# Scheduling priorities in four levels, and the FFN down weights' sums made during FFN up

## The chip, the cores and the metric

One Trainium2 chip, of which the kernel uses one core. The metric is the device time of one execution in microseconds (us), as the median of several runs. A core has the engines TensorE (PE in the rows, its weight loads PEld), VectorE (DVE), ScalarE (ACT) and GpSimd (POOL), and SyncE (SP), which here issues nearly all DMA transfers. Every engine takes its instructions in the order in which they stand in its own queue and stops at one whose inputs aren't there.

## The reference

One layer of a streaming encoder for 1024 tokens of width 1024, in float32. The change touches its last part, the gated MLP:

```python
h = rms_norm(x, norm2_w[l])
up = h @ ffn_w_up[l]                       # 1024 x 6144
gate, val = jnp.split(up, [D_FF], axis=-1) # D_FF = 3072
gate = causal_depthwise_conv(gate, ffn_conv_w[l], ffn_conv_b[l])
x = x + (jax.nn.gelu(gate) * val) @ ffn_w_down[l]
return rms_norm(x, norm_f_w)
```

Ahead of it stand a norm, an input projection of width 8192, a retention branch and a recurrent branch (RG-LRU) with an output projection each, a gated merge, and a projection with a residual.

## The kernel before

**Products.** Every large matrix product is made of jobs. A job takes a weight block of 1024 x 256 (four tiles A11, A12, A21, A22 of 128 x 512) and an operand of 1024 x 1024 (tiles B11 to B22, each in four pieces of 128 x 512). Each float32 tile is split in two (`split`, L164): ScalarE casts a high part (L167), VectorE subtracts it for the low part (L168), and each product is three passes of matmuls. A plain job (`mm_std`) has 96 matmuls. Most jobs are fast ones (`mm_fast`, L377), by Strassen's scheme in Winograd's form: 7 products of 12 matmuls, in the order A11·B11, S1·T1, S2·T2, A12·B21, S3·T3, A22·T4, S4·B22, where S1 to S4 are sums of weight tiles and T1 to T4 sums of operand tiles (T1 = B12-B11, T2 = B22-T1, T3 = B12-B22, T4 = B21-T2). A fast job uses three banks X, Y, Z of PSUM. Where one product's result goes on in two sums, ScalarE copies the bank to SBUF (`keep`, L399, the copy is L402) before the next product adds to it; a result is finished by VectorE adding a bank to such a copy (`total`, L411, the addition is L413). The sixth and seventh products of a job come after the first of the next one.

**Weight blocks.** `preps` (L224) makes the split tiles of a job and its sums S1 to S4 (L246, L249, L255, L262) from raw tiles that `loads` (L199) brings by SP (L208). `pump` keeps up to seven blocks and six raw tiles ready, from 22 tiles W of their own.

**Operands.** Generators in a queue `builders` load an operand's pieces, split them and form T1 to T4. `operand` (L983) does the 16 plain pieces, `tsets` (L539) loads the same 16 again and subtracts (L544, L547, L550, L552), one piece j of all of T1 to T4 after the other. `build` (L285) advances them after every product by a budget of 3, if 20 of the 81 tiles U are free; `need` (L295) forces them where TensorE's instruction is written. An operand with its sums holds 64 of the 81 tiles.

**FFN.** FFN up has 24 jobs (one plain, 23 fast). After job i `post_ff(i)` (L1207) does the convolution (L1212 to L1217), the gelu (L1218) and the gating (L1219) and stores to the DRAM tile `ff_d` by GpSimd's queue (L1220). FFN down contracts over 3072 in three thirds g of 1024. There the activations from `ff_d` are the weight blocks, and the operand is a third of the down weights: `down_op(g)` (L1226) loads it from `w_dn` (L1230) and builds it with its sums. It is queued for g = 0 when job 22 of FFN up ends, later in each third's third job (`down_post`, L1311). Each third has one plain and three fast jobs; the partial results go through the DRAM tile `x1_d` (loads L1260, stores L1274; the rows call it x_d). The last third ends with the final norm.

**Order.** The program's text gives every instruction a number as its priority. A planner that runs ahead of time, with an estimate of each duration, lays down each engine's queue: whenever the engine is free in its plan, it takes the ready instruction with the lowest number. `hp()` (L161) is a context that lowers the numbers by 1500. It stands around the preparation of weight blocks (`pump`, after the first job), operand builders (`build`, `need`), `keep`'s copies, `total`'s additions, and the loads and splits of the output projection's weights (L1166). All else has its plain number: `post_ff`, the stores, and the work in the queue `back`, from which `advance` takes a budget of 1 after every product.

Of the kernel before, what the change touches and what calls it, by code (L numbers as in the profile page):

```python
# [11 lines left out]
F32 = mybir.dt.float32  # L12
# [5 lines left out]
P = 128  # L18
D = 1024
T = 1024  # L20
KT = 8
TH = 512
# [64 lines left out]
class Units:  # L87
# [11 lines left out]
    def get(self, dt=F32):  # L99
        i = self.q.popleft()  # L100
        self.count += 1
        t = self.pool.tile(self.shape, dt, tag=f"{self.name}{i}", name=f"{self.name}{i}_{self.count}")
        self.at[id(t)] = (i, t)
        return t
# [12 lines left out]
RATE = 1.0  # L117
BRATE = 3.0
RESERVE = 20
FAST_RO = 0  # L120
RO_T = 9
FAST_LO = 3
# [6 lines left out]
def tile_trunk_layer(ctx, tc, x, xt, positions, params, consts, normf, w_in, w_ro, w_lo,  # L129
# [23 lines left out]
    sg_d = pdr.tile([2, KT, P, T], F32, tag="sg", name="sg_d")  # L153
    t1_d = pdr.tile([KT, P, T], F32, tag="t1", name="t1_d")
    x1_d = pdr.tile([T, D], F32, tag="x1", name="x1_d")
    ff_d = pdr.tile([3, 8, 2, P, 4, P], F32, tag="ff", name="ff_d")

    def pc(name, i):
        return par[:, PCOL[name] + i:PCOL[name] + i + 1]

    def hp():  # L161
        return tc.high_priority(offset=1500)

    def split(src, get=get):  # L164

        hi, lo = get(F32R), get(F32R)
        S.copy(hi, src)  # L167
        V.tensor_sub(lo, src, hi.bitcast(F32))  # L168
        return hi, lo
# [114 lines left out]

    def build(budget, reserve=RESERVE):  # L285

        with hp():
            while builders and budget > 0 and len(U) >= reserve:
                c = next(builders[0], None)
                if c is None:  # L290
                    builders.popleft()
                else:
                    budget -= c

    def need(op, key):  # L295
        with hp():
            while key not in op:
                if next(builders[0], None) is None:
                    builders.popleft()
        return op[key]  # L300
# [76 lines left out]
    def mm_fast(jb, op):  # L377
        X, Y, Z = psg.get(), psg.get(), psg.get()

        def prod(bank, an, bn, first):  # L380
            pump((jb, an))
            w = jb.blk[an]
            n = 0
            for j in range(4):
                c = slice(128 * j, 128 * j + 128)
                for a, b in PASSES:
                    PE.matmul(bank, w[a][:, c], need(op, (bn, j))[b], start=first and n == 0, stop=n == 11,  # L387
                              skip_group_check=True)
                    n += 1
            W.put(*w)  # L390
            state["blocks"] -= 1
            if jb.last:
                for j in range(4):
                    drop(op.pop((bn, j)))
            pump()
            build(BRATE)
            advance(RATE)

        def keep(bank):  # L399
            u = get()  # L400
            with hp():
                S.copy(u, bank)  # L402
            return u

        def more(u, m, c):
            if jb.pre is not None and (m, c) in jb.pre:
                acc = jb.take(m, c)
                V.tensor_add(u, u, acc)
                put(acc)

        def total(u, bank, m, c):  # L411
            with hp():
                V.tensor_add(u, bank, u)  # L413
            jb.emit(m, c, u, u)

        prod(X, "A11", "B11", True)
        s1 = keep(X)
        yield
        jb.ask(0, 0)
        prod(Z, "S1", "T1", True)  # L420
        prod(X, "S2", "T2", False)
        u2 = keep(X)
        more(s1, 0, 0)
        jb.ask(1, 1)
        prod(Y, "A12", "B21", True)
        total(s1, Y, 0, 0)
        psg.put(Y)
        jb.ask(1, 0)
        prod(X, "S3", "T3", False)
        u3 = keep(X)  # L430
        more(u3, 1, 1)
        total(u3, Z, 1, 1)
        yield
        jb.ask(0, 1)
        prod(X, "A22", "T4", False)
        jb.emit(1, 0, X, None)
        psg.put(X)
        more(u2, 0, 1)
        prod(Z, "S4", "B22", False)
        total(u2, Z, 0, 1)  # L440
        psg.put(Z)

# [88 lines left out]
    def reads(fetch, keys, ahead):  # L531

        keys, got = deque(keys), deque()
        while keys or got:
            while keys and len(got) <= ahead:
                got.append(fetch(*keys.popleft()))
            yield got.popleft()
# [445 lines left out]
    def operand(op, fetch, sums=True):  # L983

        keys = [(n, j) for n in ("B11", "B21", "B12", "B22") for j in range(4)]
        for key, t in zip(keys, reads(fetch, keys, 3)):
            op[key] = split(t)
            put(t)
            yield 0.6
        if sums:  # L990
            yield from tsets(op, fetch)
# [234 lines left out]
    def down_op(g):  # L1226
        def fetch(n, j):
            t = get()
            kh, c = int(n[1]) - 1, int(n[2]) - 1
            SY.dma_start(t, w_dn[8 * g + 4 * kh + j, :, TH * c:TH * c + TH])  # L1230
            return t

        yield from operand(dop[g], fetch)

    builders.append(tsets(h2, lambda n, j: keep2[n, j]))
    NF = FF // P
    dop = [{} for _ in range(3)]

    def up_post(i):
        def fn():  # L1240
            if i == NF - 2:
                builders.append(down_op(0))
            post_ff(i)
        return fn

    run([Job(pair_src(w_up, i), h2, emit_to(gv), up_post(i), fast=i >= STD_U, last=i == NF - 1,
# [132 lines left out]
```

## Time and profile before

| | |
|---|---|
| median of 3 runs | 1673.02 us (1672.82 to 1676.43) |
| profiled execution, its own time | 1675.42 us |
| its span, first to last instruction | 1673.6 us |
| TensorE's mean granted clock | 0.994 of full speed |
| busy: PE, PEld, DVE, ACT, POOL | 97%, 80%, 77%, 53%, 2% |
| bytes read, written in HBM | 164.8 MB, 54.5 MB |

The span has these parts: input projection and both branches to about 640 us, the branches' output projections to 846, the merged projection to 950, FFN up to about 1400, FFN down to the end. An engine is busy while it executes; the time ahead of an instruction in which its engine stood still is its idle time, and the profile names who released it. Idle time matters on the engine that sets the pace. A timeline row merges instructions of one line that follow each other.

### The profile page before, as it was taken

The numbers are of one execution on the slowest core, as the hardware profiler recorded it, in microseconds if no ns is written. First come the engines' busy times: TensorE is split into PE (matmuls) and PEld (weight loads), VectorE is DVE, ScalarE is ACT, GpSimd is POOL, SyncE is SP. The second block draws the span as 40 slices with busy tenths as digits, with TensorE's granted clock in tenths as the row PEclk, the third lists the DMA queues.
The fourth block names the chain that finished last, engine by engine and source line by source line (L and its number), as shares of the span: only waits on it lengthen the run. The fifth ranks groups of instructions, "written<-read, shape, count | busy, mean of one in ns | idle before, by whom it ended". The sixth has DMA issues, their size and how long they took to land.

```text
span 1673.6 us, 21183 instructions
## 1 busy us (share of the span) xinstructions
PE 1627.2 (97%) x7224; PEld 1332.6 (80%) x7224; DVE 1289.9 (77%) x2366; ACT 886.4 (53%) x1480; POOL 40.7 (2%) x60
## 2 busy tenths in 40 slices
PE   8999999999999999999999999999999999999997
PEld 6888788888888877887778788888888887777776
DVE  8998768666888889857862796777767777878886
ACT  7654444535678877753530564444444455444554
POOL 0001000000000000000000000000000000000000
PEclk9999999999999999999999999999999999999999
DMA  7243212131333348656463022222222237687851
GB/s 293 89 154 97 86 54 89 51 95 45 113 114 105 122 140 267 210 166 232 154 209 107 32 95 82 82 82 82 89 82 82 92 122 229 224 260 243 260 193 76
DMA packets 120524, 225.97 MB, mean 135 GB/s; under 512 B 14048, under 2 KB 14176, under 8 KB 120416
## 3 DMA queue, kind: packets, MB, share of 16 engines
q1 hardware_dynamic: 116192, 210.99, 39.1%
q0 software_dynamic: 4224, 13.64, 2.1%
q8 instruction: 56, 0.92, 0.2%
q14 instruction: 52, 0.43, 0.1%
HBM read 164.80 MB, written 54.53 MB: 131 GB/s over the span
## 4 chain that ended last, share of the span: by engine, by line
PE 50%; DVE 8%; DMA 6%; ACT 3%; issue 2%; SPq 0%; DVEq 0%; ACTq 0%
PE g L387 36%; PE g L330 7%; PE g L1182 4%; DMA u<-w_dn 2%; DVE u L168 2%; PE a L814 2%; DVE w L168 1%; DMA w<-ff_d 1%; DMA x_d<-u 1%; DVE u L797 1%; ACT u L167 1%; DVE u L413 1%; DMA u<-u_d 1%; PE a L513 0%; DMA u<-w_out 0%
## 5 line engine op out<-in xcount | busy, mean ns | idle before, releaser
L387 PE MATMUL g<-u,w 128*128 128x512 f32 x5124 | 1204.7, 393 | 20.1 <-ACT u L402 9.7
L387 PEld LDWEIGHTS g<-u,w 128*128 128x128 f32 x5124 | 958.9, 188 | 224.6 <-ACT u L402 14.8
L167 ACT CAST w<-w 128x512 fp32r<-128x512 f32 x471 | 291.3, 621 | 359.7 <-PE g L387 280.6
L168 DVE TENSOR_TENSOR w<-w,w 128x512 fp32r<-128x512 f32 x471 | 322.6, 686 | 90.0 <-ACT w L167 85.4
L330 PE MATMUL g<-u,w 128*128 128x512 f32 x960 | 227.2, 394 | 2.8 <-ACT u L167 2.8
L167 ACT CAST u<-u 128x512 fp32r<-128x512 f32 x232 | 139.3, 620 | 150.1 <-DVE u L552 16.1
L330 PEld LDWEIGHTS g<-u,w 128*128 128x128 f32 x960 | 181.3, 190 | 41.9 <-ACT u L167 3.2
L168 DVE TENSOR_TENSOR u<-u,u 128x512 fp32r<-128x512 f32 x232 | 154.5, 687 | 38.8 <-ACT u L167 25.9
L413 DVE TENSOR_TENSOR u<-g,u 128x512 f32<-128x512 f32 x183 | 125.6, 686 | 57.0 <-PE g L387 43.5
L402 ACT COPY u<-g 128x512 f32<-128x512 f32 x183 | 106.4, 582 | 73.8 <-PE g L387 73.7
L1182 PE MATMUL g<-u,u 128*128 128x512 f32 x384 | 90.1, 392 | 2.5 <-ACT u L167 1.6
L1182 PEld LDWEIGHTS g<-u,u 128*128 128x128 f32 x384 | 71.3, 188 | 18.4 <-ACT u L167 2.0
L1215 DVE SCALAR_TENSOR_TENSOR u<-u,par,u 128x511 f32<-128x511 f32 (+1 forms) x96 | 71.6, 747 | 6.2 <-ACT u L1212 5.5
L1220 POOL DMA_DIRECT2D ff_d<-u x48 | 36.2, 753 | 1271.0 <-DVE u L1219 1271.0
L246 DVE TENSOR_TENSOR w<-w,w 128x512 f32<-128x512 f32 x61 | 42.1, 690 | 20.6 <-DMA w<-w_up 12.6
L814 PE MATMUL a<-u,u 128*128 128x512 f32 x192 | 48.8, 394 | 4.3 <-ACT u L167 3.5
L1184 DVE TENSOR_TENSOR u<-g,u 128x512 f32<-128x512 f32 x16 | 11.1, 691 | 49.3 <-PE g L1182 49.3
L1212 ACT ACTIVATE u<-u,par 128x512 f32<-128x512 f32 x48 | 39.1, 817 | 15.7 <-DVE u L413 15.7
L814 PEld LDWEIGHTS a<-u,u 128*128 128x128 f32 x192 | 35.5, 188 | 14.3 <-ACT u L167 5.6
L249 DVE TENSOR_TENSOR w<-w,w 128x512 f32<-128x512 f32 x61 | 42.0, 688 | 0.9
L262 DVE TENSOR_TENSOR w<-w,w 128x512 f32<-128x512 f32 x61 | 41.9, 686 | 0.4
L255 DVE TENSOR_TENSOR w<-w,w 128x512 f32<-128x512 f32 x61 | 41.8, 685 | 0.3
(173 smaller groups left out, 1151.2 us busy)
## 6 DMA issues: line engine op xcount, KB each, us to landing
w<-w_in SPq DMA_DIRECT2D x112, 256.0 KB, 2.7
w<-w_up SPq DMA_DIRECT2D x96, 256.0 KB, 2.6
u<-w_dn SPq DMA_DIRECT2D x96, 256.0 KB, 4.0
u<-x_d SPq DMA_DIRECT2D x56, 256.0 KB, 5.3
x_d<-u SPq DMA_DIRECT2D x48, 256.0 KB, 3.3
ff_d<-u POOLq DMA_DIRECT2D x48, 256.0 KB, 2.5
w<-ff_d SPq DMA_DIRECT2D x48, 256.0 KB, 3.8
u<-x SPq DMA_DIRECT2D x32, 256.0 KB, 5.3
```

The costliest lines, as they stand in the source:

```text
L167: S.copy(hi, src)
L168: V.tensor_sub(lo, src, hi.bitcast(F32))
L246: V.tensor_add(s1, a21, a22)
L249: V.tensor_sub(s1, s1, a11)
L262: V.tensor_sub(s1, a12, s1)
L330: PE.matmul(ps[h], w[a][:, c], o[b], start=n == 0, stop=n == 23)
L387: PE.matmul(bank, w[a][:, c], need(op, (bn, j))[b], start=first and n == 0, stop=n == 11, skip_group_check=True)
L402: S.copy(u, bank)
L413: V.tensor_add(u, bank, u)
L814: PE.matmul(ps, wg[g][a][:, cs], xs[k][b], start=q == 0, stop=q == 5)
L1182: PE.matmul(ps, o[a][:, 128 * t:128 * t + 128], wo[k][b], start=n == 0, stop=n == 23)
L1215: V.scalar_tensor_tensor(c[:, s:], src[:, :TH - s], w, c[:, s:], ALU.mult, ALU.add)
```

## The change

`hp` takes its offset as an argument, and there are four levels beside the plain one: 3000 (NOW) for `keep`'s copies and `total`'s additions, 1500 as before for weight blocks and the output projection's weights, 800 (OLD) for `post_ff` of the last three jobs of FFN up, 400 (SOON) for the operand builders.

The sums of the down weights move. After every second job of FFN up `down_sums(g, j)` is queued in `back`, 12 in all: it loads four tiles of `w_dn`, makes the four sums and stores them to a new DRAM tile `td_d`. `down_op` loads and splits the 16 plain pieces as before, and then, in the order T1, T2, T3, T4, loads the 16 sums from `td_d` and splits them, with a budget of 0.6 for each piece where the four pieces of one j had 4.8 together.

```diff
+NOW, SOON, OLD = 3000, 400, 800
+    td_d = pdr.tile([3, 4, 4, P, TH], F32, tag="td", name="td_d")
-    def hp():
-        return tc.high_priority(offset=1500)
+    def hp(offset=1500):
+        return tc.high_priority(offset=offset)
@@ build, need
-        with hp():
+        with hp(SOON):
@@ keep, total
-            with hp():
+            with hp(NOW):
@@ down_op
-        yield from operand(dop[g], fetch)
+        yield from operand(dop[g], fetch, False)
+
+        def sums(n, j):
+            t = get()
+            SY.dma_start(t, td_d[g, int(n[1]) - 1, j])
+            return t
+
+        keys = [(f"T{i}", j) for i in (1, 2, 3, 4) for j in range(4)]
+        for key, t in zip(keys, reads(sums, keys, 3)):
+            dop[g][key] = split(t)
+            put(t)
+            yield 0.6
+
+    def down_sums(g, j):
+
+        b = {}
+        for kh in range(2):
+            for c in range(2):
+                b[kh, c] = get()
+                SY.dma_start(b[kh, c], w_dn[8 * g + 4 * kh + j, :, TH * c:TH * c + TH])
+        yield 1.0
+        t = get()
+        V.tensor_sub(t, b[0, 1], b[0, 0])
+        ST.dma_start(td_d[g, 0, j], t)
+        put(b[0, 0])
+        yield 1.0
+        V.tensor_sub(b[0, 1], b[0, 1], b[1, 1])
+        ST.dma_start(td_d[g, 2, j], b[0, 1])
+        put(b[0, 1])
+        yield 1.0
+        V.tensor_sub(b[1, 1], b[1, 1], t)
+        ST.dma_start(td_d[g, 1, j], b[1, 1])
+        put(t)
+        yield 1.0
+        V.tensor_sub(b[1, 0], b[1, 0], b[1, 1])
+        ST.dma_start(td_d[g, 3, j], b[1, 0])
+        put(b[1, 0], b[1, 1])
@@ up_post
-            post_ff(i)
+            with hp(OLD) if i >= NF - 3 else nullcontext():
+                post_ff(i)
+            return down_sums(i // 8, i % 8 // 2) if i % 2 == 0 else None
```

(`ST` is SP here, as `GQ` is False.)

## Rows read from the trace of the kernel before

**Rows 1.** The page, busy time by engine: us (share of the span) xinstructions.

```profile
PE 1627.2 (97%) x7224; PEld 1332.6 (80%) x7224; DVE 1289.9 (77%) x2366; ACT 886.4 (53%) x1480; POOL 40.7 (2%) x60
```

**Rows 2.** Busy us by stretch (xinstructions), granted clock, DMA share, GB/s: FFN up, FFN down.

```profile
960.00:1390.00 430.00, 430.00 (x1897) 355.65 (x1896) 317.20 (x521) 215.35 (x360) 33.90 (x45) 1.00 0.28 92
1390.00:1665.50 275.50, 258.98 (x1111) 210.08 (x1109) 221.80 (x398) 131.26 (x244) 2.27 (x3) 0.98 0.65 214
```

**Rows 3.** Waits of TensorE, whole span: us in total, times, longest us.

```profile
PE g L387 <- ACT u L402: 9.7, 7, 4.0
...
PE g L387 <- DVE u L413: 4.0, 2, 2.3
PE g L387 <- ACT u L1218: 3.7, 1, 3.7
```

**Rows 4.** Timeline of TensorE, FFN down: start, us, instructions [idle before <-releaser].

```profile
1405.09 8.35 PE L387 MATMUL g<-u,w 128*128 128x512 f32 x24 [4.01 <-ACT u L402]
...
1440.50 50.96 PE L387 MATMUL g<-u,w 128*128 128x512 f32 x215 [3.71 <-ACT u L1218]
...
1493.84 3.01 PE L387 MATMUL g<-u,w 128*128 128x512 f32 x12 [1.46 <-ACT u L402]
...
1513.33 3.02 PE L387 MATMUL g<-u,w 128*128 128x512 f32 x12 [1.75 <-DVE u L413]
...
1576.13 3.02 PE L387 MATMUL g<-u,w 128*128 128x512 f32 x12 [1.07 <-ACT u L402]
...
1595.73 3.02 PE L387 MATMUL g<-u,w 128*128 128x512 f32 x12 [2.30 <-DVE u L413]
...
1624.94 34.13 PE L387 MATMUL g<-u,w 128*128 128x512 f32 x149 [1.48 <-ACT u L167]
```

**Rows 5.** Timeline of all engines, 1390 to 1405 us.

```profile
1390.04 8.50 SPq L1230 DMA_DIRECT2D u<-w_dn  x9
...
1401.87 0.69 DVE L544 TENSOR_TENSOR u<-u,u 128x512 f32<-128x512 f32 x1 [1.00 <-DMA u<-w_dn]
...
1402.73 0.62 ACT L167 CAST u<-u 128x512 fp32r<-128x512 f32 x1 [2.54 <-DVE u L1217]
...
1404.46 0.58 ACT L402 COPY u<-g 128x512 f32<-128x512 f32 x1
```

**Rows 6.** The same timeline, 1438 to 1440 us.

```profile
1438.33 0.69 DVE L246 TENSOR_TENSOR w<-w,w 128x512 f32<-128x512 f32 x1 [1.93 <-DMA w<-ff_d]
...
1439.79 0.63 ACT L1218 ACTIVATE u<-u 128x512 f32<-128x512 f32 x1 [3.34 <-DVE u L1217]
```

**Rows 7.** Busy us by stretch: behind (a), and the two changes of thirds.

```profile
1401.00:1413.30 12.30, 8.29 (x26) 6.52 (x26) 9.34 (x16) 6.92 (x13) 0.76 (x1) 0.72 0.62 211
...
1491.00:1516.00 25.00, 21.79 (x96) 17.38 (x95) 23.14 (x39) 11.58 (x20) 0.00 (x0) 1.00 0.79 258
...
1573.00:1599.00 26.00, 22.62 (x99) 18.09 (x98) 23.40 (x40) 12.52 (x23) 0.00 (x0) 1.00 0.79 260
```

**Rows 8.** Waits of TensorE, 1390 us to the end.

```profile
PE g L387 <- ACT u L402: 7.2, 4, 4.0
```

**Rows 9.** FFN up, 1000 to 1380: busy us, mean ns | idle us <-releasers.

```profile
L168 DVE TENSOR_TENSOR w<-w,w 128x512 fp32r<-128x512 f32 x140 | 96.2, 687 | 53.4 <-ACT w L167 51.5 <-PE g L387 1.4
...
L246 DVE TENSOR_TENSOR w<-w,w 128x512 f32<-128x512 f32 x20 | 13.9, 693 | 12.2 <-DMA w<-w_up 12.2
```

**Rows 10.** Timeline of SP's queue in the LRU output projection, 754 to 761 us.

```profile
754.03 5.92 SPq L997 DMA_DIRECT2D u<-u_d  x11
761.05 0.32 SPq L853 DMA_DIRECT2D u_d<-u  x1
```

**Rows 11.** The page, DMA issues: KB each, median us from issue to landing.

```profile
w<-w_up SPq DMA_DIRECT2D x96, 256.0 KB, 2.6
u<-w_dn SPq DMA_DIRECT2D x96, 256.0 KB, 4.0
```

**Rows 12.** Timeline of TensorE in the LRU output projection, around 770 us.

```profile
769.68 14.83 PE L330 MATMUL g<-u,w 128*128 128x512 f32 x51 [2.78 <-ACT u L167]
```

More of the change, by code (lines that the diff above doesn't have):

```diff
@@ L295, in need @@
     def need(op, key):
-        with hp():
+        with hp(SOON):
             while key not in op:
@@ L400, in keep @@
             u = get()
-            with hp():
+            with hp(NOW):
                 S.copy(u, bank)
@@ L411, in total @@
         def total(u, bank, m, c):
-            with hp():
+            with hp(NOW):
                 V.tensor_add(u, bank, u)
```

## The prediction, made before the changed kernel was run

> **What bounds the kernel now.** I read the page first: TensorE is busy for 97% of the span [rows 1]. The change leaves the matmuls as they are, 7224 before and after, so all there is to win is TensorE's idle time, 1673.6 - 1627.2 = 46.4 us, and what slow matmuls hide in its busy time. So the second view is the table by stretch. In FFN up, 960 to 1390 us, TensorE is busy 430.00 of 430 us and issues 1897 matmuls, 0.2267 us each: nothing to win. In FFN down, 1390 to 1665.5, it issues 1111, worth 251.8 us at that pace, and takes 275.5: 23.7 us are lost [rows 2]. The third view says whom TensorE waits for: ScalarE's copies of a bank (L402) 9.7 us, VectorE's totals (L413) 4.0, a gelu of the last up units (L1218) 3.7 [rows 3]. TensorE's timeline gives the places in FFN down: (a) 4.01 us at 1405, then 24 matmuls in 8.35 us where 24 x 0.2267 = 5.4 would do: 6.9 us; (b) 3.71 at 1440, then 215 in 50.96 where 48.7 would do: 5.9; (c) at the two changes from one third of the down weights to the next, 1.46 + 1.75 and 1.07 + 2.30: 6.6; (d) 1.48 at 1625 [rows 4]. That is 20.9 of the 23.7. Behind 1665.5 come 8 us of final norm and stores, which nothing here moves.
>
> What stands behind these gaps is an order of instructions. At (a) the copy starts at 1404.46, though TensorE, which fills its bank, had run dry at 1401.1 (1405.09 - 4.01): on ScalarE it is queued behind a cast of an operand that starts at 1402.73 after 2.54 us idle, and VectorE's sums (L544) had waited for a load of w_dn, one of nine whose issue took SP 8.50 us [rows 5]. At (b) the gelu waits 3.34 us for VectorE, which had itself stood 1.93 us before L246 for a load of ff_d [rows 6]. At (c) VectorE is full: 23.14 of 25 us and 23.40 of 26 [rows 7].
>
> **The change, part by part.** *Copies and totals of a bank first (NOW, 3000 for 1500).* Nothing is added. It returns the L402 and L413 gaps, or nothing, if in the plan the bank fills only after the cast's load has landed: then the cast goes first still, and in the real queue the copy waits as before. Before FFN down it bears on three gaps of L402, 9.7 - 7.2 = 2.5 us [rows 3, 8]; I take 1.5. For (a) the bounds are 0 and 6.9. One or two casts are all that the copy must pass, and the sums that made them late go too: I take 4.5.
>
> One part of (a) is clock. In 1401 to 1413.3, after the 4.01 us of idle, the granted clock is 0.72, a mixture of the two levels 1.2 and 2.4 GHz; in 1491 to 1516, with gaps of 1.46 and 1.75, it stays at 1.00 [rows 4, 7]. So the slow matmuls, 2.9 of the 6.9 us, come back whole if the gap falls to the size of those: closing 4.01 to 2.0 gives 4.9 us, against 3.5 if the slow part shrank with the gap. The 4.5 lies between. The Trainium skill (TensorE: Matmul & The Clock Gate, section What's actually happening) says that the clock gate knows only the two levels, and that an idle stretch puts it on the lower. By that page the term would be the 4.9, and the clock rows here agree with it.
>
> *The sums of the down weights made in FFN up.* Added there: 12 builds of 4 loads, 4 subtractions and 4 stores, 48 of each. VectorE: 48 x 0.687 = 33 us [rows 9] onto 317.2 of 430: 81%. DMA: 96 x 0.262 MB = 25 MB onto 92 GB/s x 430 us = 40 MB: the share of 0.28 becomes some 0.46 [rows 2]. SP: 96 issues of 0.32 us [rows 10], 31 us in 430. Each store also holds SP until its subtraction is done, with the loads of the weight blocks queued behind it; each subtraction holds VectorE until its loads land, with splits and totals behind it, which TensorE reads. The cover: FFN up's blocks are prepared up to seven products ahead, 7 x 12 x 0.2267 = 19 us, with six raw tiles loaded beyond, and VectorE already stands 12.2 us in 20 waits for w_up there with no gap on TensorE [rows 9]. Cost 0. If the cover went, the 48 waits at the 0.61 us of those 20 would be 29 us; I bound the cost by a quarter of it, 7 us, and the gain by 0, since TensorE has no idle time there.
>
> Removed from FFN down: 16 subtractions of each third, 11 us of VectorE, and the alternation of sum, cast and split (L544, L547 and so on) in which each waits for the other engine. Loads stay at 32 for each third, 16 of w_dn and 16 of sums in place of the second reading of w_dn, which has 96 loads in all with 4.0 us to landing [rows 11]; DMA is not relieved there. But the first product with sums (T1) now needs four tiles, where the old order ended T1 only with its fourth group. If half of the 11 us falls into the 25 us at 1491, VectorE goes from 93% to 70%, and the cause of (c) is gone. Bounds 0 and 6.6; I take 4.5. What is late next is a load: 32 loads are 8.4 MB, 33 us at the 258 GB/s of that stretch [rows 7], and they start only when the last job of a third frees its tiles.
>
> *The last three up units earlier (OLD, 800 for 0).* Nothing is added. The gelu of (b) is one of these; they now go ahead of operand builders, but still behind weight blocks (1500), and the wait for ff_d that held VectorE was for a weight block. The tiles they free earlier feed the first third's loads. Bounds 0 and 5.9; I take 3.
>
> *Operand builders later (SOON, 400 for 1500).* Casts and splits of operands, and their loads on SP, give way to the weight blocks. There are six operand sets with builders (retention out, LRU out, h2 and three thirds); the nearest price of a split that is late at full clock is (d), 1.48, so the bounds are 6 x 1.5 = 9 us of cost and, since a weight block can be the late one, 2 of gain. I take a cost of 2, and at (d) itself a gain of 0.5 of 1.5, as the copies of its neighbourhood move.
>
> Sum: 4.5 + 1.5 + 4.5 + 3 + 0.5 - 2 = 12.0 us. The profiled execution, 1675.4 us with a span of 1673.6, would become 1663.4 with a span of 1661.6. It lies 2.4 us above the median of the runs shown, 1673.0, so the forecast is 1661.0.
>
> **The rivals.** *The stalls are the DMA's, not the order's.* For it: at (a) the cast waits in the end for a load of w_dn, and these land in 4.0 us where w_up's take 2.6 [rows 11]; a plan made beforehand does not know which load will be late. Against it: at (c) VectorE is full. Then (c) alone is won and the builders' cost stays: 2.5 us, 1670.5, at the edge of what can be told.
>
> *The builders starve (slower).* One mechanism, at the three starts of a third in FFN down: weight blocks take ScalarE, VectorE and SP first, and a split that TensorE needs comes late. Its price is TensorE's wait for one operand at 770 us: 2.78 us idle, then 51 matmuls in 14.83 us where 11.6 would do, 6.1 us together [rows 12]. Three of these cost 18 us against the 12 gained: 1679. It decides when the backlog of weight blocks at the start of a third is longer than the builder's lead: for T1 that lead is 96 + 12 matmuls, 24 us; for the first B tiles it is the last job of the third before, 84 matmuls, 19 us. Against it: blocks stop at seven, and VectorE has 11 us less to do for each third.
>
> *FFN up loses its clean run.* The 7 us above: 1668. Against it: the seven products of lead.
>
> *Loads of sums wait for all stores.* If a load from the DRAM tile waited for every store to it, the first third would wait for the last third's sums. Against it: eleven loads of u_d are issued from 754.03, while a store to u_d, written earlier in the program, goes out at 761.05 [rows 10]: loads wait for the part that they read. It gets no chance of its own.
>
> **How the numbers follow.** Forecast (1656 to 1667) 0.55; all of (a) to (d) and the 2.5 us before them returned at no cost, 23.4 us, 1650: 0.05; the DMA's stalls 0.18; FFN up hurt 0.07; starved builders 0.15. The range, 1653 to 1675, leaves out most of the last case and the end of the second. About 0.2% can be told from no change, 3.3 us: 1669.7 to 1676.4. Faster: 0.55 + 0.05 and two fifths of the two cases at 1670.5 and 1668, 0.70; same 0.15, slower 0.15.
>
> **What would show it.** Right: FFN up still has TensorE at 100%, VectorE near 81% and 150 GB/s; waits of TensorE for L402 and L413 in FFN down fall below 2 us; VectorE at the change of thirds is under 80%; the clock is 1.00 behind FFN up's end. Wrong: gaps that end with L167 or L168 of operand tiles at the start of a third (builders starve); gaps in FFN up; L402 gaps of the old size with casts ahead of the copy (the DMA's stalls).

## The result, and the profile of the changed kernel

| | before | changed |
|---|---|---|
| median of 20 runs | 1673.02 us (1668.54 to 1681.41) | 1679.63 us (1674.97 to 1685.56) |
| ratio, 95% interval | | 1.0033 [1.0022, 1.0045] |
| profiled span | 1673.6 us | 1678.4 us |

The change is slower, by some 5.5 us (0.0033 x 1673; the ratio is taken from all the runs, the medians are 6.6 us apart); I had forecast 12 us faster. The matmuls are the same, so the loss is idle and slow TensorE. In the changed kernel's lines, L402 of before is L404, L413 is L415, L167 and L168 are L169 and L170, L246 is L248, L1218 is L1220. New are L1232 and L1239, the loads of the plain pieces and of the sums in `down_op`, and L1254 to L1270, `down_sums`.

First the page's busy line and three groups of its DMA issues, beside [rows 1, 11]: the loads of w_dn are 96 as before, and 48 stores of sums, and as many loads of them, are new.

```profile
PE 1630.6 (97%) x7224; PEld 1333.9 (79%) x7224; DVE 1290.3 (77%) x2366; ACT 884.5 (53%) x1480; POOL 40.6 (2%) x60
...
u<-w_dn SPq DMA_DIRECT2D x96, 256.0 KB, 3.2
...
td_d<-u SPq DMA_DIRECT2D x48, 256.0 KB, 3.4
ff_d<-u POOLq DMA_DIRECT2D x48, 256.0 KB, 2.6
```

(The 96 loads of w_dn are now 48 in FFN up and 48 in FFN down.) The table by stretch, columns as in [rows 2, 7]:

```profile
640.00:960.00 320.00, 304.82 (x1342) 246.50 (x1341) 221.86 (x390) 149.51 (x239) 0.00 (x0) 0.99 0.52 170
960.00:1390.00 430.00, 428.04 (x1884) 352.11 (x1883) 340.50 (x565) 212.77 (x356) 33.07 (x44) 1.00 0.43 141
1390.00:1665.50 275.50, 263.48 (x1124) 214.22 (x1123) 199.94 (x358) 131.97 (x247) 3.01 (x4) 0.98 0.70 229
1491.00:1516.00 25.00, 21.75 (x87) 17.51 (x88) 22.06 (x36) 15.28 (x28) 0.00 (x0) 0.93 0.88 283
1573.00:1599.00 26.00, 23.04 (x88) 18.12 (x87) 20.55 (x35) 15.63 (x28) 0.00 (x0) 0.87 0.85 281
1401.00:1413.30 12.30, 9.63 (x37) 7.25 (x36) 8.70 (x16) 8.57 (x17) 0.76 (x1) 0.90 0.81 280
```

FFN up issues 1884 matmuls where it had 1897: 13 x 0.2267 = 2.9 us lost. FFN down issues more than before in the same length. Of the 4.8 us between the two spans most stands ahead of FFN up: from 640 to 960 us the kernel before issues 1359 matmuls, the changed one 1342, 17 x 0.2267 = 3.9 us. (That stretch scatters from profile to profile, see below.) At the two changes of thirds DMA is busier (0.88 and 0.85, against 0.79), and TensorE's clock is no longer 1.00.

TensorE's waits for the copies, whole span, beside [rows 3], and from 1390 us on, beside [rows 8]: the copies, which were to go first, cost more than twice the 9.7 us of before, and 11.8 in FFN down where they cost 7.2.

```profile
PE g L389 <- ACT u L404: 20.6, 12, 3.3
...
PE g L389 <- ACT u L404: 11.8, 8, 2.9
```

TensorE's timeline from 990 us on:

```profile
992.12 412.20 PE L389 MATMUL g<-u,w 128*128 128x512 f32 x1815 [1.95 <-ACT u L404]
1404.88 3.06 PE L389 MATMUL g<-u,w 128*128 128x512 f32 x12 [0.56 <-ACT u L404]
...
1410.95 7.31 PE L389 MATMUL g<-u,w 128*128 128x512 f32 x24 [2.11 <-ACT u L404]
...
1445.78 32.96 PE L389 MATMUL g<-u,w 128*128 128x512 f32 x144 [1.22 <-ACT u L404]
...
1491.38 3.02 PE L389 MATMUL g<-u,w 128*128 128x512 f32 x12 [1.30 <-ACT u L404]
...
1498.17 4.27 PE L389 MATMUL g<-u,w 128*128 128x512 f32 x12 [2.86 <-ACT u L404]
...
1582.27 5.49 PE L389 MATMUL g<-u,w 128*128 128x512 f32 x12 [2.88 <-ACT u L404]
...
1622.76 41.09 PE L389 MATMUL g<-u,w 128*128 128x512 f32 x180 [0.16 <-ACT u L404]
```

Beside [rows 4]: (a) falls from 6.6 us to 4.2 (0.56 + 2.11, and 24 matmuls in 7.31 where a run without a gap ahead takes 5.74), (b) from 5.9 to 1.2, (d) from 1.48 to 0.16. But (c) grows from 6.6 to 10.8: 1.30 + 2.86 + 2.88, and two runs of 12 in 4.27 and 5.49 where 3.02 is usual. And there is a gap in FFN up.

What stands ahead of the late copies is in ScalarE's timeline:

```profile
991.48 0.58 ACT L404 COPY u<-g 128x512 f32<-128x512 f32 x1 [2.58 <-DMA ff_d<-u]
...
1438.41 0.62 ACT L169 CAST u<-u 128x512 fp32r<-128x512 f32 x1 [1.88 <-DMA u<-td_d]
1438.93 0.63 ACT L1220 ACTIVATE u<-u 128x512 f32<-128x512 f32 x1
...
1580.51 1.22 ACT L169 CAST u<-u 128x512 fp32r<-128x512 f32 x2 [1.46 <-DMA u<-td_d]
1581.64 0.58 ACT L404 COPY u<-g 128x512 f32<-128x512 f32 x1
```

At 991 the copy itself waits, not for its bank but for a store of `ff_d`; a copy reads nothing of `ff_d`, so what it waits for is its target, a tile U that the store still reads. The Trainium skill (DMA: Bandwidth & Descriptors, section Anatomy of one DMA — SWDGE (gpsimd) path) gives such a store about 2.0 us beside the data's own time, mostly the receipt that the last byte has landed; with 256 KB at its rate that makes an estimate of 2.6 us, and the median of 2.6 us of `ff_d<-u` above agrees. The one that the copy waits for took 5.4 us, with loads and stores of the builds beside it (the only such store from 980 to 1000 us):

```profile
ff_d<-u POOLq DMA_DIRECT2D x1, 256.0 KB, 5.4
```

At 1580 the copy stands behind a cast whose load of sums has not landed. And the last builds of sums lie in FFN down, not in FFN up, as VectorE's timeline shows: a split stands 2.53 us behind a store to `td_d`, and the last gelu of FFN up, at 1438.93, comes no earlier than the 1439.79 of [rows 6].

```profile
1431.76 0.69 DVE L1269 TENSOR_TENSOR u<-u,u 128x512 f32<-128x512 f32 x1
1434.98 0.69 DVE L170 TENSOR_TENSOR u<-u,u 128x512 fp32r<-128x512 f32 x1 [2.53 <-DMA td_d<-u]
```

### The profile page after: what moved, and what is told of

Read it like the earlier page. It is cut to its first block, busy times and chain, and to the rows that moved or that the text cites. A ratio compares the mean times of both kernels' runs of the same rounds, so it can differ in the third digit from the quotient of the medians.

```text
span 1678.4 us, 21398 instructions
## 1 busy us (share of the span) xinstructions
PE 1630.6 (97%) x7224; PEld 1333.9 (79%) x7224; DVE 1290.3 (77%) x2366; ACT 884.5 (53%) x1480; POOL 40.6 (2%) x60
## 4 chain that ended last, share of the span: by engine, by line
issue 51%; PE 41%; DMA 3%; DVE 3%; ACT 1%; SPq 0%; POOL 0%; DVEq 0%; ACTq 0%; POOLq 0%
PE g L389 36%; PE g L332 4%; PE g L365 1%; DMA u<-td_d 1%; DMA x_d<-u 1%; DVE w L170 1%; DVE u L170 1%; ACT u L169 0%; DMA u<-w_dn 0%; DMA ff_d<-u 0%; DMA u<-x_d 0%; DVE u L721 0%; ACT u L404 0%; DVE u L415 0%; DMA w<-ff_d 0%
## 5 line engine op out<-in xcount | busy, mean ns | idle before, releaser
L169 ACT CAST w<-w 128x512 fp32r<-128x512 f32 x471 | 290.5, 620 | 370.8 <-PE g L389 268.6
L170 DVE TENSOR_TENSOR w<-w,w 128x512 fp32r<-128x512 f32 x471 | 322.3, 685 | 77.7 <-ACT w L169 70.3
L169 ACT CAST u<-u 128x512 fp32r<-128x512 f32 x232 | 138.5, 619 | 133.7 <-DMA u<-w_dn 26.3
L170 DVE TENSOR_TENSOR u<-u,u 128x512 fp32r<-128x512 f32 x232 | 153.6, 686 | 50.2 <-ACT u L169 34.4
L415 DVE TENSOR_TENSOR u<-g,u 128x512 f32<-128x512 f32 x183 | 125.4, 685 | 52.9 <-PE g L389 38.7
L404 ACT COPY u<-g 128x512 f32<-128x512 f32 x183 | 106.1, 580 | 67.4 <-PE g L389 64.3
L1217 DVE SCALAR_TENSOR_TENSOR u<-u,par,u 128x511 f32<-128x511 f32 x96 | 71.7, 747 | 3.8 <-ACT u L1214 3.1
L248 DVE TENSOR_TENSOR w<-w,w 128x512 f32<-128x512 f32 x61 | 42.0, 688 | 13.3 <-DMA w<-w_up 6.3
```

The costliest lines, as they stand in the source:

```text
L248: V.tensor_add(s1, a21, a22)
L1217: V.scalar_tensor_tensor(c[:, s:], src[:, :TH - s], w, c[:, s:], ALU.mult, ALU.add)
```

## The experiments

All ratios are against the kernel before, measured beside each kernel; 0.1% is 1.7 us. One profile of a kernel is less sure than its ratio: executions of the same kernel lie up to 13 us apart, and the stretch from 640 to 960 us, ahead of FFN up, holds 1332 to 1359 matmuls in the different kernels' profiles, also where their order there is the same. I read no cost from that stretch in one profile alone.

### Each part alone

The copies' and totals' level, on the kernel before:

```diff
-            with hp():
+            with hp(3000):
                 S.copy(u, bank)
@@ total
-            with hp():
+            with hp(3000):
                 V.tensor_add(u, bank, u)
```

> The kernel before with NOW alone (keep's copies and total's additions at 3000). Prediction's theory: the L402 and L413 gaps of FFN down shrink, 4 to 9 us faster than before. Rival (the plan had put the copies there already: in the compiled ScalarE queue 181 of 183 copies keep their place): no difference, within 1.5 us of before, and the 4.0 us gap ahead of the 24 matmuls at about 1405 us is still there with its cast ahead of the copy.

Measured: 1.0008 [0.9996, 1.0020]. Gap (a) is there as in [rows 4], and so is (b):

```profile
1407.74 7.34 PE L387 MATMUL g<-u,w 128*128 128x512 f32 x24 [3.43 <-ACT u L402]
1441.29 50.65 PE L387 MATMUL g<-u,w 128*128 128x512 f32 x215 [2.87 <-ACT u L1218]
```

In the two traces 181 of the 183 copies stand at the same place in ScalarE's order. The planner must take the casts for done before the bank is full, so that no level puts the copy ahead of them (its times are not on record, only the order); on the chip the casts are late, as they wait for VectorE, and the copy stands behind them (ScalarE's timeline):

```profile
1402.62 0.62 ACT L167 CAST u<-u 128x512 fp32r<-128x512 f32 x1 [2.73 <-DVE u L544]
1405.38 0.62 ACT L167 CAST u<-u 128x512 fp32r<-128x512 f32 x1 [2.14 <-DVE u L1217]
...
1407.11 0.58 ACT L402 COPY u<-g 128x512 f32<-128x512 f32 x1
```

The level of the last up units alone (800) is still under the builders' 1500. It was not run, so what it does alone is not measured; beside builders at 1500 it is only in two kernels with the moved sums (soon1500 and late_now_old, below), which are no faster than the sums without levels.

The builders' level alone:

```diff
     def build(budget, reserve=RESERVE):
-        with hp():
+        with hp(400):
@@ need
-        with hp():
+        with hp(400):
```

> The kernel before with SOON alone (operand builders at 400). Theory 1 (builders that come later cost TensorE at the LRU output projection, where the loads and splits of w_out at 1500 now go ahead of them): 3 to 6 us slower than before, with TensorE gaps between 780 and 860 us grown by 3 to 4 us and FFN up untouched. Rival (all of the loss comes from the sums' traffic): within 1.5 us of before.

Measured: 1.0020 [1.0008, 1.0031]. FFN up stays clean, and (b) gives way to new gaps at the first third's start, two of them behind operand casts (L167):

```profile
1423.38 0.50 PE L330 MATMUL g<-u,w 128*128 128x512 f32 x1 [2.82 <-ACT u L167]
...
1444.68 5.09 PE L387 MATMUL g<-u,w 128*128 128x512 f32 x21 [2.05 <-DVE u L1270]
1451.27 42.05 PE L387 MATMUL g<-u,w 128*128 128x512 f32 x183 [1.49 <-ACT u L167]
```

The sums alone, as the changed kernel with the old levels:

```diff
-NOW, SOON, OLD = 3000, 400, 800
+NOW, SOON, OLD = 1500, 1500, 0
@@ up_post
-            with hp(OLD) if i >= NF - 3 else nullcontext():
+            with nullcontext():
                 post_ff(i)
```

> The change without its priorities (all at 1500, post_ff at 0): only the sums made in FFN up. Theory 1: equal to before up to FFN up, one gap of about 2 us at the first build near 990 us, FFN down 3 to 5 us shorter: 1 to 3 us faster than before. Rival (the sums' traffic is the loss): 3 to 6 us slower, with gaps in FFN up or longer ones at the changes of thirds.

Measured: 1.0008 [0.9999, 1.0017]. The gap in FFN up comes with the sums, again behind a store of `ff_d` (ScalarE's timeline). At the start of FFN down (a) shrinks to 1.32 us, and in the place of (b) TensorE waits 3.41 us at 1443 for a copy:

```profile
990.04 0.58 ACT L404 COPY u<-g 128x512 f32<-128x512 f32 x1 [4.68 <-DMA ff_d<-u]
```

The sum of the parts, 0.08 + 0.20 + 0.08 with nothing for the level that was not run, is 0.36%, near the 0.33% measured; that this is chance is shown further below.

### Where the builds of sums stand

On the sums alone I moved the builds: only the first (from up job 0 to 3), only the last two (jobs 20 and 22 to 15 and 17), or all twelve to jobs 2 to 13 (shown).

```diff
-            return down_sums(i // 8, i % 8 // 2) if i % 2 == 0 else None
+            return down_sums((i - 2) // 4, (i - 2) % 4) if 2 <= i < 14 else None
```

> As sums_only, with the first build alone moved, from job 0 to job 3 of FFN up. Theory (the first build takes tiles while h2's sums are made, so a bank copy gets a tile that a store to ff_d still reads): the gap of 3 us near 990 us goes, 3 to 4 us faster than sums_only, that is 0.2% faster than before. Rival (what sums_late won, it won by taking the last builds away from the start of FFN down): as sums_only, within 1.5 us, with the gap near 990 us still there or replaced.

> As sums_only, with the last two builds alone moved, from jobs 20 and 22 of FFN up to jobs 15 and 17. Theory (only the first build is at fault): as sums_only, with the gap of 3.4 us near 1443 us still there. Rival (the last builds take tiles and SP while the first third's operand is loaded): the gap near 1443 us goes, 3 us faster than sums_only.

> As sums_only, with the 12 builds one each after jobs 2 to 13 of FFN up in place of jobs 0, 2, ... 22. Theory 1 (the copy at 990 us waits because its tile was last read by a store, and free tiles are few only while h2's sums are made): the 2 us gap near 990 us is gone, FFN up has TensorE at 100%, 2 us faster than sums_only. Rival (a build costs TensorE wherever it stands, as VectorE waits for its loads): the gap moves to another place in FFN up, no faster than sums_only.

Measured: 0.9998 [0.9985, 1.0011], 1.0000 [0.9988, 1.0012] and 0.9972 [0.9961, 0.9982]. Without the first build at job 0, when the sums of h2 still hold the tiles, the gap behind the `ff_d` store is gone; without the last two at the end, the gap near 1443 is gone, while (a) is 3.77 us there. Neither gain alone is clear of noise, and 3 us or more were expected of the first. All twelve in the middle is 4.7 us faster than before. Its timeline of TensorE, the whole of FFN up in one run, and its table by stretch:

```profile
983.75 418.75 PE L389 MATMUL g<-u,w 128*128 128x512 f32 x1846 [1.56 <-DVE w L170]
1406.75 7.36 PE L389 MATMUL g<-u,w 128*128 128x512 f32 x24 [2.67 <-ACT u L404]
```

```profile
960.00:1390.00 430.00, 428.44 (x1891) 354.30 (x1890) 343.34 (x569) 216.04 (x361) 33.07 (x44) 1.00 0.47 148
```

The builds' work is all there: VectorE at 343 of 430 us, DMA at 148 GB/s. So the work is hidden, and what costs is its place. The two ends alone, 0.10 and 0.08%, do not make up the 0.36% between this kernel and the sums alone, though; with some 0.15% of uncertainty on each, how the rest divides I can't tell.

This kernel also parts the two things that the first build does at 990 us: it slows the store, and it takes tiles. From 1000 to 1170 us, beside the builds, the stores of `ff_d` are slow here too, and no copy waits for one. So a slow store is not enough; the copy must also get the tile that the store reads, as when free tiles are few.

```profile
ff_d<-u POOLq DMA_DIRECT2D x19, 256.0 KB, 4.2
```

### The changes of thirds

In the changed kernel, 12 of the 16 loads of sums of each third are left out; one loaded tile is split for all four pieces of a sum, so that casts and splits stay as many.

```diff
-        for key, t in zip(keys, reads(sums, keys, 3)):
-            dop[g][key] = split(t)
+        some = [k for k in keys if k[1] == 0]
+        for (n, _), t in zip(some, reads(sums, some, 1)):
+            for j in range(4):
+                dop[g][n, j] = split(t)
+                yield 0.6
             put(t)
-            yield 0.6
```

> The changed kernel with 12 of the 16 loads of sums of each third left out (the four pieces of T1 are all split from one loaded tile, and so on: the sums of three pieces are not used). Theory (at the changes of thirds ScalarE's copies stand behind casts that wait for loads, as 32 loads come at once): the gaps of 2.9 us near 1498 and 1582 us go with their slow matmuls, and TensorE's waits for copies in FFN down fall from 11 us below 5: 6 to 9 us faster than the changed kernel, so 0.1% to 0.2% faster than before. Rival (ScalarE itself is late, whatever the loads): the gaps stay, as the changed kernel within 2 us.

Measured: 0.9981 [0.9970, 0.9992], so 36 loads less, 12 of them in the first third, give back 0.52%, 8.7 us, of the changed kernel's time. TensorE's waits for copies from 1390 us on fall from 11.8 us to 9.0 only, where less than 5 was expected. At the changes of thirds the slow matmuls are gone, and the 10.8 us shrink to 5.0 (0.58 + 2.30 and 0.28 + 1.82), but not to nothing: five casts in a row still stand ahead of the copy on ScalarE.

```profile
1492.34 2.70 ACT L169 CAST u<-u 128x512 fp32r<-128x512 f32 x5 [0.67 <-DMA u<-td_d]
1494.94 0.57 ACT L404 COPY u<-g 128x512 f32<-128x512 f32 x1
```

So I took the down operands' casts off ScalarE:

```diff
+    def split_v(src):
+        hi, lo = get(F32R), get(F32R)
+        V.tensor_copy(hi, src)
+        V.tensor_sub(lo, src, hi.bitcast(F32))
+        return hi, lo
@@ operand
-    def operand(op, fetch, sums=True):
+    def operand(op, fetch, sums=True, split=split):
@@ down_op
-        yield from operand(dop[g], fetch, False)
+        yield from operand(dop[g], fetch, False, split_v)
-            dop[g][key] = split(t)
+            dop[g][key] = split_v(t)
```

> The changed kernel with the casts of the down operands on VectorE in place of ScalarE (96 casts for each engine's count). Theory (copies wait because casts that wait for loads stand ahead of them on ScalarE): TensorE's waits for copies in FFN down fall below 4 us, and 4 to 8 us are won against the changed kernel. Rival (whoever casts waits for the load, and VectorE's totals and splits then stand behind it): the gaps turn into waits for L413's addition or L168's splits of the same size, no time is won.

Measured: 1.0020 [1.0005, 1.0035]. That is not clear of the 1.0033 of the changed kernel. The copies' waits (here L410) fall to 8.7 us, in FFN down from 11.8 to 0.7, but the totals on VectorE (L421), which cost 0.2 in the changed kernel, now cost 12.6, all in FFN down:

```profile
PE g L395 <- DVE u L421: 12.6, 5, 4.0
PE g L395 <- ACT u L410: 8.7, 6, 2.7
```

The wait only changes engines: what frees a bank now stands behind the casts on VectorE. That it is again a wait for the burst of loads is not shown. Ahead of the longest, 3.98 us at 1515, VectorE's timeline shows no idle time from 1500 us on; with the casts it is as full at this change of thirds as in the kernel before (23.14 of 25 us):

```profile
1491.00:1516.00 25.00, 21.02 (x90) 16.89 (x89) 23.14 (x46) 4.11 (x7) 0.00 (x0) 0.97 0.81 266
```

### The levels and the late builds together

The changed kernel with the late builds; the same with the builders back at 1500; and the builders' level on the kernel before, ahead of FFN up only (shown) or, with the two numbers exchanged, from FFN up on only.

```diff
+    level = {"soon": 400}
@@ build, need
-        with hp():
+        with hp(level["soon"]):
@@ ahead of FFN up
+    level["soon"] = 1500
```

> The changed kernel with its one schedule of builds altered: the twelve builds of sums are given out by the third to the fourteenth up unit, and all levels stay. Theory (the places of the first and last builds cost about 0.35%, and the builders' level costs 0.2% of its own): 0.9985 to 1.0005 against the kernel before, that is 0.3 to 0.45% under the changed kernel, with no gap near 990 us and none near 1443. Rival (the lower level cost only through the builds that came at bad moments): 0.9965 to 0.9980.

> The changed kernel with the builders' level back at 1500 and the twelve builds of sums given out by the third to the fourteenth up unit (levels 3000 and 800 stay). Theory (the levels of the copies and of the last up units change next to nothing of what is executed): as the kernel with late builds and no levels, 0.9965 to 0.9980, about 1668 to 1670 us. Rival (one of the two levels costs something of its own once the sums are there, by putting copies whose tile is not free ahead of casts that are ready): 0.9985 to 1.0005.

> The kernel before with the builders at level 400 only up to the start of FFN up, and at 1500 from there on. Theory (the lower level costs its 0.2% where operands of the merged and LRU projections are made, from 640 to 870 us): the ratio stays where the kernel with the lower level throughout had it, 1.0015 to 1.0025, and the long run of merged-projection products starts near 861 to 862 us in place of 857.5. Rival (the cost is at the start of FFN down, where that kernel showed gaps of 2.8, 2.1 and 1.5 us): 0.9995 to 1.0007, and that run starts near 857 to 858 us.

> The kernel before with the builders at 1500 up to the start of FFN up and at 400 from there on. Theory (the cost lies ahead of FFN up): 0.9995 to 1.0007, with FFN down no longer than before. Rival (it lies at the start of FFN down): 1.0010 to 1.0022, with gaps of 1.5 to 3 us between 1400 and 1455 us whose releaser is a cast for down's operands.

Measured: 0.9992 [0.9980, 1.0004] and 0.9984 [0.9972, 0.9996]; 1.0012 [0.9998, 1.0026] and 1.0003 [0.9989, 1.0017]. The first is the answer to the change as it is: moving the builds alone takes 0.41% off it and makes a loss into no change that can be told. The last two point to the projections ahead of FFN up for the lower level's cost, though their intervals overlap and neither is told from no change. Their signs don't decide it: the long run of merged-projection products starts at 861.44 and 858.65 us, as the theory has it, but at 861.37 also where the builders are at 1500 and only the last builds moved; and low builders from FFN up on do show a gap behind a cast at the start of FFN down, the rival's sign, without its loss of time:

```profile
1417.49 0.50 PE L332 MATMUL g<-u,w 128*128 128x512 f32 x1 [2.22 <-ACT u L167]
```

But on top of late builds the levels don't help: both kernels that have them lie above the 0.9972 without, the one with the builders at 1500 not clear of noise.

### Pairs of levels

Is the lower builder level all that costs? First only it taken back in the changed kernel; then all four levels without the sums; then each pair of two levels; then all levels with the builders low from FFN up on only, without and with late sums.

```diff
@@ post_ff's level (OLD), on the kernel before with builders at 400
-            post_ff(i)
+            with hp(800) if i >= NF - 3 else nullcontext():
+                post_ff(i)
```

> The changed kernel with only the builders' level back at 1500 (levels 3000 and 800 and the early builds of sums stay). Theory (of the levels, only the builders' costs anything): as the kernel with the sums and no levels, 1.0000 to 1.0017, some 4 us under the changed kernel, with the gaps near 990 us and at the start of FFN down still there. Rival (the levels of copies and of the last up units cost too, once the sums are there): 1.0020 to 1.0040.

> The kernel before with all four levels and without the moved sums. Theory (parts add up, and only the builders' level costs): 1.0015 to 1.0027, as the kernel with that level alone. Rival (the three levels work together: with the builders low, copies and last up units gain what they could not gain alone): 0.9985 to 1.0008, with the gaps (a) and (b) of FFN down gone.

> The kernel before with the builders at 400 and the last three up units at 800, copies and totals at 1500 as before, no sums. Theory (with the builders at 400 the last up units go ahead of them, which a level of 800 cannot do while the builders are at 1500; the copies' level adds nothing): 0.9970 to 0.9992, with less than 3 us of gaps together at 1405 and 1440 us. Rival (the gain needs the copies ahead of the casts): 1.0010 to 1.0027, with the gap at 1405 still 2 us or more.

> The kernel before with copies and totals at 3000 and builders at 400, the last up units without a level, no sums. Theory (the gain is that of the last up units): 1.0010 to 1.0027, with a gap near 1440 to 1445 us behind a gelu of the last up units. Rival (it is the copies'): 0.9970 to 0.9992.

> The kernel before with all four levels, but the builders at 1500 until FFN up starts and at 400 from there on; no sums. Theory (the lower builder level costs 0.1 to 0.2% ahead of FFN up and makes room for the last up units behind it): 0.9962 to 0.9977. Rival (it costs nothing ahead of FFN up): 0.9978 to 0.9992, as with all levels throughout.

> The changed kernel with the builders at 1500 until FFN up starts, and the twelve builds of sums given out by the third to the fourteenth up unit. Theory (the levels and the late sums both take away the same stalls, those at the start of FFN down, so they don't add): 0.9960 to 0.9982. Rival (they add): 0.9935 to 0.9955. The change of thirds should still show copies behind casts, gaps of 2 to 3 us each.

| levels | sums | ratio |
|---|---|---|
| 3000, 1500, 800 (soon1500) | early | 1.0017 [1.0002, 1.0031] |
| all (no_sums) | none | 0.9982 [0.9968, 0.9996] |
| builders 400, last up units 800 (soon_old) | none | 0.9978 [0.9965, 0.9991] |
| copies 3000, builders 400 (now_soon) | none | 1.0020 [1.0007, 1.0033] |
| all, builders low only from FFN up on (ffn_levels) | none | 0.9970 [0.9955, 0.9984] |
| the same (ffn_late) | late | 0.9980 [0.9964, 0.9996] |

This overturned my account of the levels. (The first row, at the edge of its theory, decides nothing: with the builders back at 1500 the changed kernel can be told neither from the sums alone nor from the change.) Builders at 400 cost 0.20%, but with the last up units at 800 the pair gains 0.22%: together they let `post_ff` pass the builders, which the builders' level doesn't do alone. The copies' level makes no difference that can be told, 1.0020 beside 1.0020 and 0.9982 beside 0.9978. The last gelu of FFN up (ScalarE's timeline) shows the passing: in no_sums, in soon_old and in now_soon, in this order:

```profile
1417.66 0.63 ACT L1218 ACTIVATE u<-u 128x512 f32<-128x512 f32 x1 [1.02 <-DVE u L1217]
```

```profile
1421.72 0.63 ACT L1218 ACTIVATE u<-u 128x512 f32<-128x512 f32 x1 [1.01 <-DVE u L1217]
```

```profile
1444.99 0.63 ACT L1218 ACTIVATE u<-u 128x512 f32<-128x512 f32 x1
```

It was at 1439.79 before [rows 6]. With all levels and no sums, (a) and (b) are nearly gone from TensorE's timeline, and the stretch of [rows 7] behind (a), 0.72 there, runs at full clock with 54 matmuls for 26:

```profile
1400.82 3.02 PE L387 MATMUL g<-u,w 128*128 128x512 f32 x12 [1.15 <-ACT u L402]
...
1437.39 14.80 PE L387 MATMUL g<-u,w 128*128 128x512 f32 x64 [0.59 <-ACT u L402]
1453.84 32.10 PE L387 MATMUL g<-u,w 128*128 128x512 f32 x140 [1.65 <-DVE u L413]
```

```profile
1401.00:1413.30 12.30, 12.30 (x54) 9.73 (x55) 11.47 (x20) 7.27 (x14) 0.76 (x1) 1.00 0.78 276
```

The kernel with low builders only from FFN up on is 5.0 us faster than before, the best beside the late sums without levels. Four pairs of kernels now differ in nothing but the builders' level ahead of FFN up: throughout or from there on only (1.0020 and 1.0003), the same with all levels (0.9982 and 0.9970) and with late sums too (0.9992 and 0.9980), and up to there only or not at all (1.0012 and 1). The low level is the slower one in all four, by 0.12 to 0.17%; no pair alone is clear of noise. Late sums and levels together (0.9980) do not add, which would give 0.994: they take away the same stalls, those at the start of FFN down, and the sums leave their own, 3.39 us at 1441 and 2.6 us at each change of thirds.

So the changed kernel's loss has this composition. The levels alone gain 0.18%. The sums on top cost 0.51% (1.0033 against 0.9982), and 0.41% of that goes with the builds' places. The last builds put their four loads, sums and stores exactly where the levels had cleared the way, so that the last gelu falls back from 1417.66 to 1438.93. With all levels and late builds (late_all) it is back:

```profile
1418.28 0.63 ACT L1220 ACTIVATE u<-u 128x512 f32<-128x512 f32 x1
```

The 0.52% of the 36 loads is not a further part: with fewer loads and the last builds where they were, that gelu comes at 1424.75, so the two ways out share at least this stall. No run has both, and how far they overlap is open.

## Why the prediction failed, step by step

**The start held.** TensorE is the bound, nothing in FFN up was to be won, and FFN down was the place: it did gain, 16 matmuls more by 1660 us (1104 against 1088), 3.6 us (both counted from 1390 us). What it gained was lost ahead of it, in FFN up (2.9 us) and before (3.9, in a stretch that scatters). FFN up's load came as worked out: VectorE 340.5 of 430 us (79%, 81% forecast), 141 GB/s (150 forecast).

**The builds at cost 0: the step that failed most.** The cover that I named, seven products of weight blocks, was real, and it was the wrong one. The first build didn't starve a weight block. It took five tiles U while h2's sums held theirs, and a copy then got a tile that a store was still reading. (The wait shows the second half; how many tiles were free at that moment was not counted.) I counted durations and queues, not tiles. In FFN up that is the 2.9 us. And I took "in FFN up" from the text of the change: the last builds, queued behind job 22, have their sums at 1428 to 1432 us, in FFN down. My bound for this term was 7 us; moving the builds gave back 0.41%, 6.9 us. The value taken was wrong, and that the bound fits is luck: it was a quarter of 29 us, a share that no row gave, for a wait that didn't occur.

**Copies first: 4.5 + 1.5 forecast, nothing measured** (1.0008 alone; 1.0020 with the builders' level, as without it). I had written down the case, that the plan has the bank full only after the cast, and gave it the end of the range. It was the case here: a level can only choose between instructions that are ready in the plan at the same time.

**Last up units: 3 forecast, and 7 us measured** for the pair's second half (1.0020 to 0.9978); alone it was not run. My words were that they "now go ahead of operand builders", which was right, and I costed the two levels apart although one works only through the other.

**Builders later: -2 forecast, -3.3 measured** (0.20%). The range held it. The place was wrong: I put the starving at the three starts of a third; the kernel with the low level from FFN up on only is at 1.0003. The four pairs above put it ahead of FFN up, at 0.12 to 0.17%.

**The change of thirds: 4.5 forecast, 4.2 lost.** VectorE did get relief, less than forecast (22.06 of 25 us and 20.55 of 26, 88% and 79%, where it had 23.14 and 23.40 and I forecast 70%), and it was not the bound: the four-level kernel without the sums has VectorE at 25.34 of 26 us in its last change of thirds and gaps of only 1.44 and 0.35.

```profile
1568.00:1594.00 26.00, 24.21 (x106) 19.38 (x105) 25.34 (x43) 13.63 (x25) 0.00 (x0) 1.00 0.80 272
```

What I had named as "late next", the burst of 32 loads, is what came, and I gave it no price. Leaving out 36 loads, those of the first third among them, gives one: up to 8.7 us.

**The clock step held in part.** With gaps of 2.86 and 2.88 us the matmuls behind fell to 12 in 4.27 and 5.49 us, and in the kernel where the gap of (a) is 1.15 us, the clock is 1.00. The granted clock over those 5.49 us is 0.50, the lower of the two levels, and 5.49 is about twice the 2.72 of 12 matmuls at full pace; 4.27 lies between. But that the slow part comes back whole once the gap is down to about 2 us did not hold: behind the 2.11 us at 1411, 24 matmuls still took 7.31 us in place of 5.74.

**The rivals.** That the stalls are the DMA's named the sign that appeared (copies behind casts, at the old size) but gave 1670.5. The starved builders gave 1679, near the measured time, for another reason. FFN up losing its clean run had the place of the first build, at a price (7 us) that FFN up alone did not lose, and I set it against gains that didn't come. No case had two parts that cost each other's gain, which is what happened.

## What to carry to other kernels

A scheduling level does something only against what it passes: before costing it, find the instruction that it is to overtake, and ask whether both are ready at that moment in the plan and which level the other has. Work that is moved to an idle stretch needs tiles and a deadline there, beside engine time: check what holds the buffers when it starts, and whether its last piece ends before the stretch does. And parts of a change whose gains lie at the same stall are neither additive nor testable one by one; run the pairs.

## What the runs showed of the hardware that I had not expected

A copy between PSUM and SBUF can stand for a transfer: 2.58 us at 991 us in the changed kernel and 4.68 us with the sums alone, for a store that took 5.4 and 5.6 us to land where the median is 2.6.

A long row of SP's timeline is not a slow issue. I read the 8.50 us of [rows 5] in the prediction as the time that nine issues took, but a merged row holds the waits between them too. Single issues of that row, and of the loads of sums in the burst at the second change of thirds of the changed kernel, take 0.32 to 0.43 us (ns, least, median and most, first and last start). In between SP stands, at least in part for tiles that TensorE has yet to free. What grows in the burst is the time to land, 5.7 us in median at 281 GB/s, where a load of w_dn takes 2.9 in FFN up at 141 GB/s:

```profile
L1230 SPq DMA_DIRECT2D u<-w_dn x9: 328/382/430, 1390.0 to 1398.2; - x9
...
L1239 SPq DMA_DIRECT2D u<-td_d x8: 319/356/391, 1573.2 to 1580.3; - x8
...
DMA to landing us min/median/max: 3.6/5.7/6.0
```

And the size of a gap alone doesn't tell whether the matmuls behind it keep their pace: behind gaps of 1.86 and 1.98 us (the kernels with the first or the last builds moved) 12 matmuls took 4.60 us, behind 2.25 and 2.36 us in the same kernels 3.02.
